# Matmuls of 512 columns issued as two of 256, with output weights moved modulo 256 bytes, in a two-layer encoder kernel

## The chip, the cores and the metric

The kernel runs on one core of a Trainium2 chip, in one launch. The metric is the device time in microseconds. Three runs of the kernel before took 1810.51, 1814.37 and 1808.48 us; their median, 1810.51 us, is the time to compare with. One execution was also profiled, and it is the source of every row shown.

## The reference

Two groups of 512 tokens of width 1024 (a prompt group and a sample group) go through the same two layers and a final norm. Layer 0 is differential attention with 8 heads, layer 1 is retention in both directions with 8 heads. Both layers have one wide input projection that also yields a gate, and one output projection. All is computed in float32.

```python
def trunk(x, ...):
    h = rms_norm(x, norm_g[0]);  x = x + diff_attention(h, da_w_in, ..., da_w_out)
    h = rms_norm(x, norm_g[1]);  x = x + bidir_retention(h, ret_w_in, ..., ret_w_out)
    return rms_norm(x, final_norm_g)

# diff_attention, per head: two softmaxes over 512 keys, a difference of them, times v,
#   rms_norm per head, times silu(gate), then o @ w_out
# bidir_retention, per head: (q k^T * decay) v forwards and backwards in chunks,
#   rms_norm per head, times silu(gate), then o @ w_out
```

## The kernel before

TensorE gets float32 precision from a rounded type (float32r): each operand is split into a high part and a low part, and each product is made of three passes, high by high, high by low and low by high (PASSES). A matmul in this text is one such pass: it loads 128 x 128 weights (the stationary operand, second argument of the call) and streams the moving operand (third argument) past them, up to 512 columns, into one bank of PSUM of 512 float32 columns. In the profile, PE is the matmul and PEld the load of its weights; each matmul has a load of its own.

The stages are these, with the lines of the profile:

- Input projections of both layers. They use a scheme with seven products in place of eight (P1 to P7), over the two groups and two halves of the depth. A Unit of kind "pair" makes its products in pair(), L599: the weights are a working tile ws of prepared projection weights, and the moving operand is a B tile of normalised activations, 512 columns wide. A Unit of kind "wide" does it the other way round, L609: the weights are a B tile, the moving operand is ws, 256 columns wide.
- Attention scores, L1116: weights are q, the moving operand is k, 512 columns. Transposes of probabilities, L1161. Attention times v, L1181: 256 columns.
- Retention: scores L1315, states L1339, near and far outputs L1359 and L1367, all of 256 columns.
- Output projections of both layers, out_step, L891: the weights are the tiles oT that hold the gated head output, the moving operand is ws with the prepared output weights, 512 columns. The very last output tile is made in two parts of 256 columns. L896 adds the product to the running x.
- Transposes for norms and layouts: L716, L815, L1028.

The work is recorded as operations with costs in a planner (Plan), which then fixes one order for each engine. The costs are written into the code and the change leaves them as they are. Each operation of TensorE is a whole group of matmuls, for instance the 12 of pair() or the 6 of out_step, and other engines wait for the end of a group. PSUM has eight banks under four tags, pj (3), sc (2), o (2) and tp (1).

SBUF is laid out in this order in each partition: small columns (pool sm), constants and B tiles (cp), the arena (ar) and working tiles (wk: raw, ws, st, os, c, e, m). The arena is one tile of 18 slots of 1024 floats, with a lead of 32 floats. slot() hands out slots, and its shift moves a tile some floats further. Tiles with the same shift lie at the same place modulo 256 bytes, since a slot is 4096 bytes. Work tiles that are not a multiple of 16 floats wide go into sm. ssf is such a tag: it has 12 columns of sums of squares that square() and x_norm() use in turn.

Of the kernel before, what the change touches and what calls it, by code (L numbers as in the profile page):

```python
# [9 lines left out]
F32 = mybir.dt.float32  # L10
F32R = mybir.dt.float32r
# [4 lines left out]
P = 128  # L16
S = 512
# [236 lines left out]
def trunk_kernel(  # L254
# [7 lines left out]
    nc = tc.nc  # L262
# [4 lines left out]
    sm = ctx.enter_context(tc.tile_pool(name="sm", bufs=1))  # L267
    cp = ctx.enter_context(tc.tile_pool(name="cp", bufs=1))
    ar = ctx.enter_context(tc.tile_pool(name="ar", bufs=1))
# [7 lines left out]
    places = {}  # L277
    cnt = [0]

    def view(pool, tag, i, size, shape, dt=F32):  # L280


        if size % 16 and pool in (cp, wk):
            pool = sm
        if (tag, i) not in places:
            places[tag, i] = pool.tile([P, size], F32, tag=f"{tag}{i}", name=f"{tag}_{i}", bufs=1)
        n = math.prod(shape[1:])
        t = places[tag, i][0:shape[0], 0:n]
        if dt != F32:
            t = t.bitcast(dt)  # L290
        if len(shape) == 3:
            t = t.rearrange("p (a b) -> p a b", a=shape[1])
        elif len(shape) == 4:
            t = t.rearrange("p (a b c) -> p a b c", a=shape[1], b=shape[2])
        return t

    def work(tag, shape, bufs, dt=F32, name=None):
        size = SIZE.get(tag, shape[1])
        return Buf(plan, tag, bufs, lambda i: view(wk, tag, i, size, shape, dt))

    arena = ar.tile([P, 18 * 1024 + 80], F32R, tag="arena", name="arena")

    def slot(n, shape, dt=F32R, shift=0):

        size = math.prod(shape[1:])
        at = None if n in (12, 13) or n >= 20 else n if n < 12 else n - 2
        if at is None:
            assert not shift  # L310
            cnt[0] += 1
            label = f"b_{cnt[0]}"
            return Buf(plan, f"b{n}", 1, lambda i: cp.tile(shape, dt, tag=f"b{n}", name=label))
        assert dt == F32R
        lo = 32 + at * 1024 + shift

        def make(i):
            t = arena[:, lo:lo + size]
            return t.rearrange("p (a b) -> p a b", a=shape[1]) if len(shape) == 3 else t
        b = Buf(plan, f"b{n}", 1, make)  # L320
        b.also = Buf(plan, f"edge{at + 1 if shift else at}", 1, None)
        return b

    def const(shape, tag, dt=F32, size=None):
        return Buf(plan, tag, 1, lambda i: view(cp, tag, i, size or math.prod(shape[1:]), shape, dt))
# [27 lines left out]
    def bank(tag, name=None):  # L353
        return Buf(plan, tag, BUFS[tag], lambda i: view(pj if tag == "pj" else sc, tag, i, S, [P, S]))
# [19 lines left out]
    def axpy(n, fn, r, w):  # L374

        plan.op("DVE", 0.13 + 0.00104 * n, fn, r, w)
# [13 lines left out]
    def pe(cost, fn, r, w, wait=0.0):  # L390
        plan.op("PE", cost, fn, r, w, wait=wait)
# [126 lines left out]
    class Unit:  # L518
# [67 lines left out]
        def product(self, op):  # L586
            which = BANK_OF[op]
            n_banks = 2 if self.wide else 1
            opens = op in OPENS
            if opens:  # L590
                self.banks[which] = [bank(self.tags[which], which) for _ in range(n_banks)]
            a, b = self.ops.pop(op), B_OF[op]
            bt = [Bop[b, k] for k in range(4)]
            reads = [q[1] for q in a] + bt

            def pair(ps, ks=range(4)):
                for k in ks:
                    for i, (u, v) in enumerate(PASSES):
                        nc.tensor.matmul(  # L599
                            ps.t, a[u][0]()[:, k, :], bt[k][:, v, :], start=(opens and k == 0 and i == 0),  # L600
                            stop=(k == 3 and i == 2), skip_group_check=True)

            def wide(ps, t):
                if self.led and op == "P1" and t == 0:
                    for j in range(NT):
                        nc.tensor.transpose(ps[:, j * P:(j + 1) * P], ident.t, ident.t)
                for k in range(4):
                    for i, (u, v) in enumerate(PASSES):
                        nc.tensor.matmul(  # L609
                            ps[:, (t % 2) * 256:(t % 2) * 256 + 256], bt[k][:, v, t * P:(t + 1) * P],  # L610
                            a[u][0]()[:, k, :], start=(opens and t % 2 == 0 and k == 0 and i == 0),
                            stop=(k == 3 and i == 2), skip_group_check=True)

            if not self.wide:
                ps = self.banks[which][0]
                if op == "P1" and self in first_units[:2]:
                    for k in range(4):
                        pe(0.7, lambda k=k: pair(ps, (k,)), reads[:2] + [bt[k]], [(ps, k)])
                else:
                    pe(2.79, lambda: pair(ps), reads, [ps])  # L620
                return
            for t in range(NT):
                ps = self.banks[which][t // 2]
                led = self.led and op == "P1" and t == 0
                pe(1.87 if led else 1.43, lambda ps=ps, t=t: wide(ps, t), reads + [ident] * led, [ps])
# [198 lines left out]
        return rr  # L824

    def new_oT(g):
        return [slot(16 + 2 * g + a, [P, 2, S], F32R, 32) for a in range(2)]

    def load_qk(src, i, shift):
        t = slot(i, [P, 2, S], F32R, shift)  # L830
# [31 lines left out]
    def out_weights(w, h, i):  # L862
        r = raw_t([P, 2, S])
        src = w[h * 256:(h + 1) * 256, i * S:(i + 1) * S].rearrange("(e p) c -> p e c", p=P)
        dma(lambda: r.t, lambda: src, [], [r], 512)
        hi, lo = ws_t([P, 2, S]), ws_t([P, 2, S])
        hi_of(1024, lambda: hi.t, lambda: r.t, [r], [hi])
        lo_of(1024, lambda: lo.t, lambda: r.t, lambda: hi.t, [r, hi], [lo])
        wsn[h, i] = (hi, lo)

    def out_step(w, h, g, t, i, o, rr, last, parts=1):


        owed[h, g] -= 1
        if (h, i) not in wsn:
            out_weights(w, h, i)
        banks = [bank("pj") for _ in range(parts)]
        u = wsn[h, i]
        x = xN[g, t]
        n = S // parts  # L880
        for p in range(parts):
            here = slice(p * n, (p + 1) * n)
            part = (x, i) if parts == 1 else (x, (i, p))

            ps = banks[p]

            def fn(here=here, ps=ps):
                m = 0
                for e in range(2):
                    for a, b in PASSES:  # L890
                        nc.tensor.matmul(ps[:, here], o[a][:, e, t * P:(t + 1) * P], u[b][:, e, here],  # L891
                                         start=(m == 0), stop=(m == 5))
                        m += 1
            pe(1.39 / parts, fn, [(o[0], t // 2), (o[1], t // 2), *u], [ps])
            half = x[:, i * S + p * n:i * S + (p + 1) * n]
            axpy(n, lambda half=half, here=here, ps=ps: nc.vector.scalar_tensor_tensor(  # L896
                half, ps[:, here], rr[:, t % 2:t % 2 + 1], half, op0=ALU.mult, op1=ALU.add),
                [ps, part, rr], [part])
            if h == NH - 1:
                last(g, t, i, half, n, part, i == 1 and p == parts - 1)  # L900
# [206 lines left out]
    def scores(i):  # L1107
        h, g, t = tiles[i]
        st[i]['s'] = []
        for j in range(2):  # L1110
            s = bank("sc")
            q, k = qk[h, g, j, 0], qk[h, g, j, 1]

            def fn(s=s, q=q, k=k):
                for n, (a, b) in enumerate(PASSES):
                    nc.tensor.matmul(s.t, q[:, a, t * P:(t + 1) * P], k[:, b, :], start=(n == 0), stop=(n == 2))  # L1116
            pe(0.7, fn, [q, k], [s])
            st[i]['s'].append(s)

# [229 lines left out]
    def av2(b, c):  # L1349
# [29 lines left out]
        if c == 0:  # L1379
            settle(h - 1, g)  # L1380
            oT[h, g] = new_oT(g)
# [71 lines left out]
    for i in range(N2 + 1):  # L1453
        if i < N2:
            b, c = chunks[i]
# [78 lines left out]
```

## Time and profile before

| what | before |
|---|---|
| median of three runs | 1810.51 us (1808.48 to 1814.37) |
| the profiled execution, first to last instruction | 1807.0 us |
| instructions | 27780 |
| matmuls, and as many loads of weights | 10299 |
| moved by DMA | 328.81 MB, mean 182 GB/s |

The span of the profiled execution leaves out what lies around its first and last instruction; the median of the runs is 3.5 us above it.

A row of the page's first part gives an engine, its busy time, its share of the span and its number of instructions. A row of a group gives line, engine, operation, what it writes and reads, the shape and the count, then the busy time in us and the mean of one in ns, then the idle time before it and what ended that. A row of the timeline gives the start in us, the length in us, the engine, line and operation, and how many instructions of one kind were merged. The end of a matmul is modelled, so lengths overlap the next row; starts are what to compare. A row of waits gives who waited for whom, the time in total, the number of times and the longest.

### The profile page before, as it was taken

How to read it: one execution, taken by the hardware profiler on the slowest of the kernel's cores; microseconds unless marked ns; L12 is line 12 of the kernel's file. 1: busy time of each engine (PE TensorE's matmuls, PEld its weight loads, DVE VectorE, ACT ScalarE, POOL GpSimd, SP SyncE). 2: the span in 40 equal slices, each digit the busy share in tenths (PEclk: the TensorE clock that was granted, in tenths of full speed). 3: DMA queues.
4: the chain of work that ended last, by engine and by line, in shares of the span. 5: the costliest groups of instructions: out<-in, count | busy, mean ns of one | idle time of the engine just before them, and what ended most of it. 6: DMA issues, size and time to landing. Idle time of an engine off the chain costs nothing.

```text
span 1807.0 us, 27780 instructions
## 1 busy us (share of the span) xinstructions
PE 1794.9 (99%) x10299; PEld 1558.1 (86%) x10299; DVE 1477.1 (82%) x2319; ACT 895.1 (50%) x1856; POOL 169.5 (9%) x323
## 2 busy tenths in 40 slices
PE   9999999999999999999999999999999999999998
PEld 6789889898988888888888888898989898888887
DVE  7958787778699888888888897787887967888887
ACT  7753444433434565554555866444434355444346
POOL 1000000000000022222322300000000000111113
PEclk9999999999999999999999999999999999999999
DMA  6444455555545685444554524464657559765662
GB/s 217 134 126 137 161 140 178 184 168 155 174 126 175 201 334 198 178 156 159 190 204 140 190 73 146 140 210 146 205 156 228 151 170 396 272 238 182 225 218 94
DMA packets 162767, 328.81 MB, mean 182 GB/s; under 512 B 12724, under 2 KB 76872, under 8 KB 162632
## 3 DMA queue, kind: packets, MB, share of 16 engines
q1 hardware_dynamic: 162304, 326.71, 54.1%
q8 instruction: 81, 1.33, 0.3%
q14 instruction: 54, 0.44, 0.1%
q10 hardware_dynamic: 328, 0.34, 0.1%
HBM read 209.55 MB, written 117.44 MB: 181 GB/s over the span
## 4 chain that ended last, share of the span: by engine, by line
PE 93%; DVE 2%; DMA 2%; ACT 2%; issue 1%; POOL 0%; SPq 0%; POOLq 0%; DVEq 0%; ACTq 0%
PE pj L599 20%; PE pj L891 19%; PE sc L599 10%; PE pj L609 10%; PE o L599 8%; PE o L1181 5%; PE sc L1116 5%; PE sc L609 5%; PE o L609 2%; PE o L1359 2%; PE tp L1161 2%; PE sc L1315 1%; PE o L1367 1%; PE tp L1339 1%; DMA raw<-in_ret_w_out_dram 1%
## 5 line engine op out<-in xcount | busy, mean ns | idle before, releaser
L891 PE MATMUL pj<-ws,arena 128*128 128x512 f32 x1542 | 391.2, 397 | 0.0
L891 PEld LDWEIGHTS pj<-ws,arena 128*128 128x128 f32 x1542 | 277.7, 188 | 52.7
L599 PE MATMUL pj<-b,ws 128*128 128x512 f32 x1080 | 265.0, 392 | 0.0
L599 PEld LDWEIGHTS pj<-b,ws 128*128 128x128 f32 x1080 | 201.4, 188 | 43.0
L403 DVE TENSOR_TENSOR ws<-st,ws 128x512 fp32r<-128x512 f32 (+1 forms) x192 | 147.9, 774 | 74.8 <-ACT ws L400 56.7
L896 DVE SCALAR_TENSOR_TENSOR b<-pj,crr,b 128x512 f32<-128x512 f32 (+1 forms) x257 | 189.9, 744 | 21.4 <-PE pj L891 21.0
L403 DVE TENSOR_TENSOR ws<-raw,ws 128x512 fp32r<-128x512 f32 (+1 forms) x164 | 141.5, 868 | 71.3 <-ACT ws L400 61.0
L400 ACT CAST ws<-st 128x512 fp32r<-128x512 f32 (+1 forms) x192 | 132.4, 693 | 121.4 <-PE pj L599 36.4
L599 PE MATMUL sc<-arena,ws 128*128 128x512 f32 x768 | 186.8, 392 | 0.0
L599 PE MATMUL o<-arena,ws 128*128 128x512 f32 x744 | 180.0, 393 | 1.1 <-ACT m L385 0.6
L599 PEld LDWEIGHTS sc<-arena,ws 128*128 128x128 f32 x768 | 144.0, 188 | 31.3
L400 ACT CAST ws<-raw 128x512 fp32r<-128x512 f32 (+1 forms) x164 | 125.7, 772 | 87.0 <-PE o L599 45.0
L599 PEld LDWEIGHTS o<-arena,ws 128*128 128x128 f32 x744 | 138.4, 188 | 31.7 <-DVE arena L463 1.4
L599 PE MATMUL pj<-arena,ws 128*128 128x512 f32 x648 | 160.3, 392 | 0.4 <-DVE arena L463 0.4
L599 PEld LDWEIGHTS pj<-arena,ws 128*128 128x128 f32 x648 | 120.8, 188 | 26.7 <-DVE arena L463 0.7
L1134 ACT ACTIVATE b<-sc,nm 128x512 f32<-128x512 f32 x128 | 88.0, 689 | 66.9 <-DVE nm L1124 66.5
L636 ACT COPY c<-pj 128x512 f32<-128x512 f32 x104 | 60.9, 586 | 119.7 <-PE pj L599 66.4
L609 PE MATMUL pj<-ws,b 128*128 128x256 f32 x960 | 116.8, 276 | 0.0
L609 PEld LDWEIGHTS pj<-ws,b 128*128 128x128 f32 x960 | 113.2, 188 | 0.7
L1116 PE MATMUL sc<-arena 128*128 128x512 f32 x384 | 101.2, 395 | 0.3 <-ACT b L1134 0.3
L1181 PEld LDWEIGHTS o<-arena 128*128 128x128 f32 x768 | 93.1, 188 | 2.7
L1181 PE MATMUL o<-arena 128*128 128x256 f32 x768 | 93.7, 278 | 0.0
(207 smaller groups left out, 2855.9 us busy)
## 6 DMA issues: line engine op xcount, KB each, us to landing
qk<-os SPq DMA_DIRECT2D x192, 256.0 KB, 3.6
arena<-qk SPq DMA_DIRECT2D x96, 512.0 KB, 5.8
raw<-in_da_w_in_dram SPq DMA_DIRECT2D x64, 512.0 KB, 5.1
v<-os SPq DMA_DIRECT2D x64, 512.0 KB, 4.3
arena<-v SPq DMA_DIRECT2D x64, 512.0 KB, 4.1
raw<-in_ret_w_in_dram SPq DMA_DIRECT2D x48, 512.0 KB, 4.8
os<-g SPq DMA_DIRECT2D x32, 512.0 KB, 7.4
g<-e SPq DMA_DIRECT2D x48, 256.0 KB, 4.6
```

Of the source, the lines that this page charges most:

```text
L400: act(n, lambda: nc.scalar.copy(dst(), src()), r, w)
L403: dve(n, lambda: nc.vector.tensor_tensor(dst(), src(), hi().bitcast(F32), op=ALU.subtract), r, w)
L599: nc.tensor.matmul(ps.t, a[u][0]()[:, k, :], bt[k][:, v, :], start=(opens and k == 0 and i == 0), stop=(k == 3 and i == 2), skip_group_che ...
L609: nc.tensor.matmul(ps[:, (t % 2) * 256:(t % 2) * 256 + 256], bt[k][:, v, t * P:(t + 1) * P], a[u][0]()[:, k, :], start=(opens and t % 2 == ...
L636: act(S, lambda c=c, ps=ps: nc.scalar.copy(c.t, ps.t), [ps], [c])
L891: nc.tensor.matmul(ps[:, here], o[a][:, e, t * P:(t + 1) * P], u[b][:, e, here], start=(m == 0), stop=(m == 5))
L896: axpy(n, lambda half=half, here=here, ps=ps: nc.vector.scalar_tensor_tensor(half, ps[:, here], rr[:, t % 2:t % 2 + 1], half, op0=ALU.mult ...
L1116: nc.tensor.matmul(s.t, q[:, a, t * P:(t + 1) * P], k[:, b, :], start=(n == 0), stop=(n == 2))
L1134: act(840, lambda j=j, s=s, m=m: nc.scalar.activation(p[:, j, :], s.t, AF.Exp, bias=m.t, accum_out=sm[:, 2 * j + n:2 * j + n + 1]), [s, m] ...
L1161: nc.tensor.transpose(tp[:, j * P:(j + 1) * P], p[:, 0, j * P:(j + 1) * P], ident.t)
L1181: nc.tensor.matmul(o[:, e * 256:(e + 1) * 256], v[b][:, j, e * P:(e + 1) * P], aT[a][:, j, :], start=(n == 0), stop=(n % 12 == 11), skip_g ...
L1359: nc.tensor.matmul(o[:, e * 256:(e + 1) * 256], v_[v][:, 2 * c + j, e * P:(e + 1) * P], a_[:, u, j * 256:(j + 1) * 256], start=(e == 0 and ...
```

## The change

There are three edits of matmuls, one of places and one that makes room.

In pair(), out_step() and scores(), each matmul of 512 columns is issued as two of 256, one after the other, with the same weights and the two halves of the moving operand, into the two halves of the same bank. Only the first of them opens the bank. Each loads its weights again. The eight matmuls that run before the first work keep their 512 columns.

The tiles oT get a shift of 64 floats in place of 32, and the arena grows by 64 floats, that is 256 bytes. The 12 columns ssf are packed in one tile of 32 columns, which takes 128 bytes in place of 12 times 32, so that sm shrinks by 256 bytes. Constants, B tiles and the arena's start move by 256 bytes, and everything behind the arena stays where it was. Modulo 256 bytes only the tiles oT and the small columns behind ssf lie elsewhere.

```diff
         if size % 16 and pool in (cp, wk):
             pool = sm
+            if tag == "ssf":
+                if tag not in places:
+                    places[tag] = sm.tile([P, 16 + 16], F32, tag=tag, name=tag, bufs=1)
+                return places[tag][:, i:i + 1]
...
-    arena = ar.tile([P, 18 * 1024 + 80], F32R, tag="arena", name="arena")
+    arena = ar.tile([P, 18 * 1024 + 144], F32R, tag="arena", name="arena")
...
                 for k in ks:
                     for i, (u, v) in enumerate(PASSES):
-                        nc.tensor.matmul(
-                            ps.t, a[u][0]()[:, k, :], bt[k][:, v, :], start=(opens and k == 0 and i == 0),
-                            stop=(k == 3 and i == 2), skip_group_check=True)
+                        for c in range(2):
+                            here = slice(c * 256, (c + 1) * 256)
+                            nc.tensor.matmul(
+                                ps[:, here], a[u][0]()[:, k, :], bt[k][:, v, here],
+                                start=(opens and k == 0 and i == 0 and c == 0),
+                                stop=(k == 3 and i == 2), skip_group_check=True)
...
     def new_oT(g):
-        return [slot(16 + 2 * g + a, [P, 2, S], F32R, 32) for a in range(2)]
+        return [slot(16 + 2 * g + a, [P, 2, S], F32R, 64) for a in range(2)]
...
                 for e in range(2):
                     for a, b in PASSES:
-                        nc.tensor.matmul(ps[:, here], o[a][:, e, t * P:(t + 1) * P], u[b][:, e, here],
-                                         start=(m == 0), stop=(m == 5))
+                        for c0 in range(here.start, here.stop, 256):
+                            nc.tensor.matmul(
+                                ps[:, c0:c0 + 256], o[a][:, e, t * P:(t + 1) * P], u[b][:, e, c0:c0 + 256],
+                                start=(m == 0 and c0 == here.start), stop=(m == 5), skip_group_check=True)
                         m += 1
...
                 for n, (a, b) in enumerate(PASSES):
-                    nc.tensor.matmul(s.t, q[:, a, t * P:(t + 1) * P], k[:, b, :], start=(n == 0), stop=(n == 2))
+                    for c in range(2):
+                        here = slice(c * 256, (c + 1) * 256)
+                        nc.tensor.matmul(s[:, here], q[:, a, t * P:(t + 1) * P], k[:, b, here],
+                                         start=(n == 0 and c == 0), stop=(n == 2), skip_group_check=True)
```

## The prediction

> **What bounds the kernel now.** I read the page first, then the groups of TensorE by form, then TensorE's waits, then its timeline, because the question is how fast one matmul follows another.
>
> ```profile
> span 1807.0 us, 27780 instructions
> PE 1794.9 (99%) x10299; PEld 1558.1 (86%) x10299; DVE 1477.1 (82%) x2319; ACT 895.1 (50%) x1856; POOL 169.5 (9%) x323
> PEclk9999999999999999999999999999999999999999
> PE 93%; DVE 2%; DMA 2%; ACT 2%; issue 1%; POOL 0%; SPq 0%; POOLq 0%; DVEq 0%; ACTq 0%
> q8 instruction: 81, 1.33, 0.3%
> ```
>
> TensorE is busy from end to end at the full granted clock, and 93% of the chain that ended last is its own work. Its longest waits, with one for a memset at the very start, are tiny:
>
> ```profile
> PE sc L1010 <- DVE minus L411: 1.4, 1, 1.4
> PE tp L1028 <- DVE arena L463: 1.0, 2, 0.7
> ```
>
> So the time is a sum of steps from one matmul's start to the next one's. The "mean ns of one" in a group is no such step: it covers the whole passage of one matmul, and matmuls overlap. What the groups give is the counts:
>
> ```profile
> L891 PE MATMUL pj<-ws,arena 128*128 128x512 f32 x1530 | 389.8, 398 | 0.0
> L599 PE MATMUL pj<-b,ws 128*128 128x512 f32 x1080 | 265.0, 392 | 0.0
> L599 PE MATMUL sc<-arena,ws 128*128 128x512 f32 x768 | 186.8, 392 | 0.0
> L599 PE MATMUL o<-arena,ws 128*128 128x512 f32 x744 | 180.0, 393 | 1.1 <-ACT m L385 0.6 <-DVE arena L463 0.3
> L599 PE MATMUL pj<-arena,ws 128*128 128x512 f32 x648 | 160.3, 392 | 0.4 <-DVE arena L463 0.4
> L1116 PE MATMUL sc<-arena 128*128 128x512 f32 x384 | 101.2, 395 | 0.3 <-ACT b L1134 0.3
> L599 PE MATMUL sc<-b,ws 128*128 128x512 f32 x120 | 29.1, 391 | 0.0
> L891 PE MATMUL pj<-ws,arena 128*128 128x256 f32 x12 | 1.6, 280 | 0.0
> ```
>
> L599 has 1080 + 768 + 744 + 648 + 120 = 3360 matmuls of 512 columns, L891 1530 and L1116 384: 5274 are split, and 5274 matmuls, each with its own load of weights, are added.
>
> **The step of a 512 against two of 256.** In the timeline the start of the next row less the start of a row, over the row's count, is the step. Two long unbroken stretches, each by its first and last row and the row after:
>
> ```profile
> 450.94 5.63 PE L609 MATMUL o<-ws,arena 128*128 128x256 f32 x48
> ...
> 472.72 5.61 PE L609 MATMUL pj<-ws,b 128*128 128x256 f32 x48
> 478.16 2.91 PE L599 MATMUL pj<-arena,ws 128*128 128x512 f32 x12
> 486.38 2.91 PE L599 MATMUL o<-arena,ws 128*128 128x512 f32 x12
> ...
> 625.08 1.53 PE L599 MATMUL pj<-arena,ws 128*128 128x512 f32 x6
> 626.46 0.86 PE L1116 MATMUL sc<-arena 128*128 128x512 f32 x3
> ```
>
> L609: 240 matmuls in 478.16 - 450.94 = 27.22 us, 113.4 ns each. L599: 612 in 626.46 - 486.38 = 140.08 us, 228.9 ns each. Two of 256 columns at L609's step are 226.8 ns, 2.1 less than one of 512. That is the small thing this change can win, and it is multiplied by thousands. But a 256 also leaves less time for the load of the next weights, and other lines of 256 show that the step isn't always 113.4:
>
> ```profile
> 640.45 2.92 PE L599 MATMUL pj<-b,ws 128*128 128x512 f32 x12
> 643.21 2.89 PE L1181 MATMUL o<-arena 128*128 128x256 f32 x24
> 645.93 0.85 PE L1116 MATMUL sc<-arena 128*128 128x512 f32 x3
> 650.87 3.01 PE L891 MATMUL pj<-ws,arena 128*128 128x512 f32 x12
> 653.72 2.99 PE L1181 MATMUL o<-arena 128*128 128x256 f32 x24
> 656.55 0.86 PE L1116 MATMUL sc<-arena 128*128 128x512 f32 x3
> 1548.49 0.86 PE L1339 MATMUL tp<-arena 128*128 128x256 f32 x6
> 1549.19 0.87 PE L1315 MATMUL sc<-arena 128*128 128x256 f32 x6
> 1549.89 1.54 PE L891 MATMUL pj<-ws,arena 128*128 128x512 f32 x6
> 1551.27 1.52 PE L1359 MATMUL o<-arena 128*128 128x256 f32 x12
> 1552.63 0.84 PE L1367 MATMUL o<-arena,b 128*128 128x256 f32 x6
> 1553.31 1.55 PE L891 MATMUL pj<-ws,arena 128*128 128x512 f32 x6
> 1554.70 0.38 PE L815 MATMUL tp<-ident,m 128*128 128x128 f32 x2
> ```
>
> L1181 takes 2.72 us for 24 in one group (113.3 ns) and 2.83 in another (117.9). L1339 and L1315 take 0.70 for 6 (116.7), L1359 1.36 for 12 and L1367 0.68 for 6 (113.3 both). The last of L891, already of 256 columns, show (1.6 - 0.28) / 11 = about 120 ns. Beside this I set where each line's weights begin, modulo 256 bytes, by the allocation of the program: 32 for L609, L1359 and L1367 (all fast), 96 for L1181 and L1339 (fast or slow), 160 for L1315 and L891 (slow). The moving operand's place (32, 96 or 224) doesn't sort them. So I read two steps of a stream of 256s, a short one of 113.4 and a long one of about 117.7 ns, and the weights' place decides which one holds.
>
> **The change part by part.**
>
> *Weights of L891.* The tiles that new_oT makes start 32 floats further, and the arena itself starts 256 bytes earlier. Their place goes from 160 to 32 modulo 256; the moving operand stays at 224. That is exactly L609's pair, so I take 113.4 ns. The 512 of today:
>
> ```profile
> 688.76 1.54 PE L1116 MATMUL sc<-arena 128*128 128x512 f32 x6
> 690.14 2.92 PE L891 MATMUL pj<-ws,arena 128*128 128x512 f32 x12
> 692.90 0.60 PE L1161 MATMUL tp<-ident,b 128*128 128x128 f32 x4
> ```
>
> 12 in 2.76 us are 230.0; the groups of six at 1549.89 and 1553.31 take 1.38 and 1.39, 230.0 and 231.7. I take 230.5. Gain: (230.5 - 226.8) x 1530 = 5.7 us. Bounds: at 113.0 a half 6.9 us are won; at 117.7 4.9 x 1530 = 7.5 us are lost.
>
> *L1116.* Weights at 32, moving at 96, as L1359 has them. Today 1.38 us for 6, 230.0 each; gain 3.2 x 384 = 1.2 us.
>
> *L599.* Its weights are the working tiles ws, at 224 modulo 256, which the change leaves alone, and no line of 256 columns has its weights there. This is the unknown price, and the largest count: 113.4 gives 2.1 x 3360 = 7.1 us won, 117.7 gives 6.5 x 3360 = 21.8 us lost. I take 113.4. For it: where L599 follows L609, as at 478.16 and 486.38, it takes over a fast stream; and L1181's group at 643.21, behind L599, was fast, while the one at 653.72, behind L891, was slow. Against it: 32, 96, 160 grow worse in that order, and 224 is the next. It is a judgement, not a reading.
>
> *Columns of sums of squares.* Twelve tiles of one column become one of 32 columns: 128 bytes a partition in place of 384, which pays for the arena's 256 more, so that every tile behind the arena keeps its address. In the built program the order of ACT, DVE, POOL and SP is unchanged, and POOL and SP wait as before. DVE gets 14 more instructions that only wait, for events of long ago; even at the 744 ns of a whole pass of L896 (the page's group of that line) they would be 10 us of the 330 that DVE is idle.
>
> ```profile
> L896 DVE SCALAR_TENSOR_TENSOR b<-pj,crr,b 128x512 f32<-128x512 f32 (+1 forms) x257 | 189.9, 744 | 21.4 <-PE pj L891 21.0
> ```
>
> I cost them at nothing, covered by TensorE's own work. Instructions are fetched by a queue that is busy 0.3% of the time; half as many again change nothing there.
>
> *Sum.* 7.1 + 5.7 + 1.2 = 14.0 us. I hand back 1.5: a stream needs some matmuls to fall into the fast step after a change of line (L1339's six lose 3.3 ns each), and an engine that is 0.8% faster will wait a little more for DVE, which has 18% to spare. Net 12.5 us. The profiled span of 1807.0 becomes 1794.5; the median of the runs, 1810.51, is 3.5 above that span, so 1798. Own range 1792 (halves at 113.0 and L1181 always fast) to 1804 (half the gain).
>
> **The rivals.**
>
> *The long step at L599.* Loads of weights come twice as often; at 224 they end last, and L599 runs as L1315 and the slow L1181 do. The price is 21.8 us against the 6.9 that L891 and L1116 win: +15, 1825. It decides from a step of 114.5 ns at L599 upward. For it stands that the place isn't measured; against it that a fast stream stays fast. 0.22. If 224 were worse still, 120 ns as L891's last twelve, 11.1 x 3360 = 37 us are lost: 1841. 0.03.
>
> *In between.* L599 flips as L1181 does, mean 115.5: 2.1 x 3360 = 7 us lost, 6.9 won: 1810. 0.09.
>
> *The shift does nothing.* L891 stays at 117.7 because place isn't the cause: +7.5 - 7.1 - 1.2 = -0.8, 1810. The fast rows at 32 speak against it. 0.03. The Trainium skill, "TensorE: Matmul & The Clock Gate" (Step-by-step: what each phase is for), says that loading weights and streaming use two independent read ports and that the load takes no bandwidth from the running matmul. By that rule alone the shift would do nothing; L1359 against L1315 here speaks against it.
>
> *A fixed cost per matmul.* Whatever sets L599's 228.9 is per column, and each further matmul costs something, as L1181's slow groups do: half of those 6.5 ns more on all 5274 is +17, 1828. Two of 256 were cheaper than one of 512 at L609, so 0.03. The same page (Back-to-back issue gap) gives N / 2.4 + 2.5 ns for a step, by which two of 256 cost 2.5 ns more than one of 512, an estimate of 13 us for the 5274, 1824. The trace differs: 228.9 and 113.4 where the rule has 215.8 and 109.2, and the pair is cheaper.
>
> **How the numbers follow.** Forecast 0.60, rivals 0.22 + 0.03 + 0.09 + 0.03 + 0.03. A difference under 0.3% (5.4 us) can't be told from no change. Faster: 0.60. Same: in between and the idle shift, 0.12. Slower: 0.28. The range 1791 to 1826 takes in the long step; left out are the worse place, half of the fixed cost and the edges of the forecast.
>
> **What would show it.** In the new timeline the long stretch of L599's line should step at 113.4 ns (0.68 us for 6), L891's line the same, L1116's too; the busy share of the weight loads goes from 86% to nearly all, and TensorE's waits stay a few us. L599 at 0.70 to 0.71 us for 6 is the long step. I am wrong altogether if TensorE shows idle time behind DVE, or if both steps stay and the time moves.

## The result, and the profile after

| | before | after |
|---|---|---|
| median | 1809.49 us (4 runs, 1808.26 to 1814.37) | 1833.66 us (4 runs, 1832.97 to 1836.69) |
| ratio to before, 95% interval | | 1.0137 (1.0124 to 1.0150) |
| span of the profiled execution | 1807.0 us | 1831.8 us |

The changed kernel is 1.4% slower. The forecast was 1798.0 us, and its range ended at 1826. Lines have moved: L599 is now L605, L609 is L616, L891 is L899, L1116 is L1127, L1181 is L1193, L1359 is L1371, L1367 is L1379.

The page of the kernel after, its head, chain and instruction queue:

```profile
span 1831.8 us, 38342 instructions
PE 1819.5 (99%) x15573; PEld 1810.2 (99%) x15573; DVE 1480.0 (81%) x2319; ACT 895.3 (49%) x1856; POOL 169.3 (9%) x323
PEclk9999999999999999999999999999999999999999
q8 instruction: 122, 2.00, 0.5%
PE 95%; DVE 2%; DMA 1%; issue 1%; ACT 1%; POOL 0%; SPq 0%; POOLq 0%; DVEq 0%; ACTq 0%
```

TensorE's longest waits, after:

```profile
PE sc L1019 <- DVE minus L415: 1.4, 1, 1.4
PE o L1037 <- DVE b L391: 1.1, 1, 1.1
```

Nothing came in from outside TensorE. It is as busy as before at the same granted clock, its waits are of the same size, instructions are fetched by a queue that is busy 0.5% of the time, and 15573 - 10299 = 5274 matmuls were added as counted. So the 24.8 us lie in the steps. Adding up, over the whole trace, the time from each matmul's start to the next one's, and giving it to the line of the first, shows where:

| line before / after | before, us | after, us | difference | taken in the prediction |
|---|---|---|---|---|
| L599 / L605 | 774.3 | 787.8 | +13.5 | -7.1 |
| L609 / L616 (not split) | 305.7 | 309.9 | +4.2 | 0 |
| L891 / L899 | 362.1 | 363.9 | +1.8 | -5.7 |
| L1116 / L1127 | 89.8 | 91.9 | +2.1 | -1.2 |
| L1181 / L1193 (not split) | 88.4 | 89.6 | +1.2 | 0 |
| L1359 / L1371 (not split) | 43.7 | 45.3 | +1.6 | 0 |
| L1367 / L1379 (not split) | 22.2 | 22.6 | +0.4 | 0 |

The differences add up to 24.8, the whole change of the span. Lines that nobody touched pay 7.4 of it.

The timeline shows what happened inside a line (start, length, count; the step is the distance of starts over the count):

```profile
196.78 5.82 PE L616 MATMUL pj<-ws,b 128*128 128x256 f32 x48
202.44 2.99 PE L605 MATMUL o<-arena,ws 128*128 128x256 f32 x24
...
292.90 2.99 PE L605 MATMUL pj<-b,ws 128*128 128x256 f32 x24
295.72 5.62 PE L616 MATMUL pj<-ws,arena 128*128 128x256 f32 x48
301.17 2.89 PE L605 MATMUL pj<-b,ws 128*128 128x256 f32 x24
303.89 5.82 PE L616 MATMUL o<-ws,arena 128*128 128x256 f32 x48
...
490.36 5.62 PE L616 MATMUL pj<-ws,b 128*128 128x256 f32 x48
495.81 2.88 PE L605 MATMUL o<-arena,ws 128*128 128x256 f32 x24
...
633.17 1.52 PE L605 MATMUL pj<-arena,ws 128*128 128x256 f32 x12
634.53 0.85 PE L1127 MATMUL sc<-arena 128*128 128x256 f32 x6
```

From 202.44 to 295.72 L605 runs 792 matmuls in 93.28 us, 117.78 ns each. From 495.81 to 634.53 the same line, with its weights at the same place modulo 256, runs 1224 in 138.72 us, 113.33 ns each. Neither step gives way to the other while the stream lasts. L616, with weights at 32, does both too: (202.44 - 196.78) / 48 = 117.9 ns, (301.17 - 295.72) / 48 = 113.5 ns. So one line has both steps with its weights at one place, and the place alone can't be what decides. The rows suggest that it is how a stream was entered, which the experiments below test. In the rows above, L616 takes the other step than the L605 ahead of it (long to short at 295.72, short to long at 303.89), and L605 keeps the step of the L616 ahead of it. Over the trace, the change from L605 to L616 turned the step round 19 times of 23, and the change from L616 to L605 kept it 24 times of 24. As the lines alternate, an unbroken stretch then has the one step or the other by the number of changes before it. Of L605's matmuls 1781 took 112 to 115 ns and 4909 took 116 to 124; of L616's 1614 and 1069, where before 2554 of them were short and 129 long.

The same timeline where output products alternate with scores, and with the far outputs:

```profile
697.68 1.58 PE L1127 MATMUL sc<-arena 128*128 128x256 f32 x12
699.09 2.89 PE L899 MATMUL pj<-ws,arena 128*128 128x256 f32 x24
701.82 0.60 PE L1173 MATMUL tp<-ident,b 128*128 128x128 f32 x4
...
1543.83 1.58 PE L1371 MATMUL o<-arena 128*128 128x256 f32 x12
1545.24 0.86 PE L1351 MATMUL tp<-arena 128*128 128x256 f32 x6
```

L899 runs at (701.82 - 699.09) / 24 = 113.8 ns here, but L1127 at 1.41 / 12 = 117.5, and L1371, for which the prediction had 113.3, at 1.41 / 12 = 117.5 as well. The weights of all three lie at 32, which the prediction had called the good place. Over the whole trace L899 is mixed, with 1367 matmuls of 112 to 115 ns and 1609 of 116 to 124, L1127 is long in 730 of its 768, and L1371 in all of its 384.

### The profile page after: what moved, and what is told of

Read it like the earlier page. It is cut to its first block, busy times and chain, and to the rows that moved or that the text cites. A ratio compares the mean times of both kernels' runs of the same rounds, so it can differ in the third digit from the quotient of the medians.

```text
span 1831.8 us, 38342 instructions
## 1 busy us (share of the span) xinstructions
PE 1819.5 (99%) x15573; PEld 1810.2 (99%) x15573; DVE 1480.0 (81%) x2319; ACT 895.3 (49%) x1856; POOL 169.3 (9%) x323
## 4 chain that ended last, share of the span: by engine, by line
PE 95%; DVE 2%; DMA 1%; issue 1%; ACT 1%; POOL 0%; SPq 0%; POOLq 0%; DVEq 0%; ACTq 0%
PE pj L605 21%; PE pj L899 19%; PE sc L605 11%; PE pj L616 10%; PE o L605 8%; PE o L1193 5%; PE sc L1127 5%; PE sc L616 5%; PE o L1371 2%; PE o L616 2%; PE tp L1173 2%; PE sc L1327 1%; PE o L1379 1%; PE tp L1351 1%; DVE ws L407 0%
## 5 line engine op out<-in xcount | busy, mean ns | idle before, releaser
L899 PE MATMUL pj<-ws,arena 128*128 128x256 f32 x3072 | 393.1, 281 | 0.0
L899 PEld LDWEIGHTS pj<-ws,arena 128*128 128x128 f32 x3072 | 369.3, 189 | 0.1
L605 PE MATMUL pj<-b,ws 128*128 128x256 f32 x2160 | 269.3, 279 | 0.0
L605 PEld LDWEIGHTS pj<-b,ws 128*128 128x128 f32 x2160 | 259.2, 188 | 0.0
L905 DVE SCALAR_TENSOR_TENSOR b<-pj,crr,b 128x512 f32<-128x512 f32 (+1 forms) x257 | 190.2, 745 | 22.6 <-PE pj L899 21.2
L605 PE MATMUL sc<-arena,ws 128*128 128x256 f32 x1536 | 189.9, 279 | 0.0
L605 PE MATMUL o<-arena,ws 128*128 128x256 f32 x1488 | 183.6, 279 | 1.0 <-ACT m L389 0.6
L605 PEld LDWEIGHTS sc<-arena,ws 128*128 128x128 f32 x1536 | 183.7, 188 | 0.0
L605 PEld LDWEIGHTS o<-arena,ws 128*128 128x128 f32 x1488 | 177.9, 188 | 1.9 <-DVE arena L467 1.1
L605 PE MATMUL pj<-arena,ws 128*128 128x256 f32 x1296 | 162.3, 278 | 0.3 <-DVE arena L467 0.3
L605 PEld LDWEIGHTS pj<-arena,ws 128*128 128x128 f32 x1296 | 155.5, 188 | 0.7 <-DVE arena L467 0.5
L616 PE MATMUL pj<-ws,b 128*128 128x256 f32 x960 | 118.6, 278 | 0.0
L616 PEld LDWEIGHTS pj<-ws,b 128*128 128x128 f32 x960 | 114.3, 188 | 0.0
L1127 PE MATMUL sc<-arena 128*128 128x256 f32 x768 | 103.4, 281 | 0.3 <-ACT b L1146 0.3
L1127 PEld LDWEIGHTS sc<-arena 128*128 128x128 f32 x768 | 95.5, 188 | 0.7 <-ACT b L1146 0.7
L1193 PE MATMUL o<-arena 128*128 128x256 f32 x768 | 94.8, 280 | 0.0
```

The lines of the kernel that those rows point to most:

```text
L605: nc.tensor.matmul(ps[:, here], a[u][0]()[:, k, :], bt[k][:, v, here], start=(opens and k == 0 and i == 0 and c == 0), stop=(k == 3 and i ...
L616: nc.tensor.matmul(ps[:, (t % 2) * 256:(t % 2) * 256 + 256], bt[k][:, v, t * P:(t + 1) * P], a[u][0]()[:, k, :], start=(opens and t % 2 == ...
L899: nc.tensor.matmul(ps[:, c0:c0 + 256], o[a][:, e, t * P:(t + 1) * P], u[b][:, e, c0:c0 + 256], start=(m == 0 and c0 == here.start), stop=( ...
L1127: nc.tensor.matmul(s[:, here], q[:, a, t * P:(t + 1) * P], k[:, b, here], start=(n == 0 and c == 0), stop=(n == 2), skip_group_check=True)
L1193: nc.tensor.matmul(o[:, e * 256:(e + 1) * 256], v[b][:, j, e * P:(e + 1) * P], aT[a][:, j, :], start=(n == 0), stop=(n % 12 == 11), skip_g ...
```

## The experiments

All kernels here compute the whole reference. A "whole" matmul has 512 columns, a "half" is one of the two of 256 that replace it, and a "product" is the group of twelve whole matmuls that one call of pair() makes. "Short" is the step of 113.3 ns for 256 columns, "long" the step of 117.8. Sums by line are made as in the table above and are named by the lines of before; rows of a timeline have the lines of their own kernel. The ratios are formed from all runs, so they can differ a little from the ratio of the medians.

**One edit at a time.** Four kernels take the change apart, with hunks of the change itself. e1_pair_only is the kernel before with the hunk of pair(). e2_pair_whole is the change without that hunk. e3_place_only is the kernel before with ssf in one tile, the longer arena and the shift, and no split; e4_split_old_place is the change without these (the hunk of ssf is the one shown with the change):

```diff
...
-    arena = ar.tile([P, 18 * 1024 + 80], F32R, tag="arena", name="arena")
+    arena = ar.tile([P, 18 * 1024 + 144], F32R, tag="arena", name="arena")
...
-        return [slot(16 + 2 * g + a, [P, 2, S], F32R, 32) for a in range(2)]
+        return [slot(16 + 2 * g + a, [P, 2, S], F32R, 64) for a in range(2)]
```

> Only pair() is split, everything else as before. Theory A (a stream of 256s has a short step of 113.4 ns and a long one of 117.7 that both hold by themselves; a change of line hands the step on or flips it): the split line has a mix of both, mean 116.6 as in the changed kernel, and L609, which is untouched, loses too, mean about 115; (2 x 116.6 - 229.0) x 3360 = 14 us and 1.5 x 2688 = 4 us, so 1828 (1820 to 1835). Theory B (the weights' place modulo 256 sets the step): the split line has the long step throughout, (235.4 - 229.0) x 3360 = 21 us, 1831, and L609 stays at 113.6 ns. Theory C (twice the instructions starve TensorE): waits without a releaser at TensorE, and L609 as before.

> The changed kernel with pair() left at 512 columns. Theory A: the rest of the loss, 24 - 18 = 6 us, so about 1815; L609 back at 113.6 ns since each L599 product of 512s stands before it; L1359 and L1367 long as in the changed kernel. Theory B: the out_step line, its weights now at 32, is short throughout, and 5.7 + 1.2 us are won, 1803.

> Only the places: oT moved to 32 modulo 256, ssf packed, no matmul split. Theory A and C: 512s do not feel the place, 1809 to 1811. Theory B: the twelve last 256s of L891 are short, 0.05 us, else the same.

> All three splits, but oT and ssf where they were before, weights of L891 at 160 modulo 256. Theory A: the place does not set the step, only what a change of line does with it: the out_step line has a mix of both steps, time within 10 us of the changed kernel, 1824 to 1844. Theory B: the out_step line is long throughout (117.7 ns against 115.7 in the changed kernel), 4 x 1530 = 6 us more, 1840, and L609 keeps what it has in the changed kernel.

| | median, us (before 1808.60) | ratio, 95% interval | L599 | L609 | L891 | L1116 | L1359 |
|---|---|---|---|---|---|---|---|
| e1_pair_only | 1826.42 | 1.0093 (1.0078 to 1.0108) | 784.3 | 312.7 | 362.2 | 89.9 | 43.7 |
| e2_pair_whole | 1816.36 | 1.0045 (1.0030 to 1.0060) | 773.9 | 305.7 | 363.9 | 91.9 | 45.2 |
| e3_place_only | 1813.94 | 1.0029 (1.0017 to 1.0040) | 774.8 | 305.9 | 365.5 | 89.7 | 45.1 |
| e4_split_old_place | 1833.97 | 1.0143 (1.0128 to 1.0158) | 780.6 | 312.7 | 367.9 | 91.7 | 45.2 |

The two parts of the change add up: 1.0093 and 1.0045 to 1.0137. Splitting pair() alone costs 10.0 us in L599 and 7.0 in L609, which it does not touch; theory A had 14 and 4, and with 1828 and 1815 it was near the times of e1_pair_only and e2_pair_whole, where theory B had 1831 with L609 unchanged, and 1803. The places alone are not free, which neither theory had: the matmuls of 512 columns at L891 lose 3.4 us, and L1359, whose own operands stay where they were modulo 256, turns long. With the splits, the new places give L891 4.0 us (367.9 against 363.9; 1609 of its matmuls long against 2535 at the old place, nearly as theory B had that line), but L599 and L609 together take 4.4 more, and the whole time stays the same, where theory B had 1840. The timeline of e3_place_only, whose L1363 is L1359 of before:

```profile
1551.49 1.55 PE L895 MATMUL pj<-ws,arena 128*128 128x512 f32 x6
1552.88 1.57 PE L1363 MATMUL o<-arena 128*128 128x256 f32 x12
1554.30 0.87 PE L1371 MATMUL o<-arena,b 128*128 128x256 f32 x6
```

Twelve of L1363 take 1.42 us, 118.3 ns, where before they took 1.36 behind the same six output products. The trace shows what turned L1359: of its 29 groups behind L891 in before, the 28 that came behind a last step of 235 or 236 ns were short and the one behind 226 was long; in e3_place_only 28 came behind 230 or 231 and were long, and one behind 235 was short. So the places changed the steps of L891, and with its last step went the step of the line behind it. Whether the packed ssf had a share in the 0.3% was not tried by itself.

**Twice the same weights, or 512 as a fresh start?** The first two passes of pair() both load the high part of ws, and the third the low part. So in the change four of every six halves follow one with the same weights. In e5_halves_outside it is two of six, not none as its expectation says. In e6_last_whole the twelfth matmul of each product stays whole, and in e7_last_split only the twelfth is split, 280 matmuls in all, so that the halves are few and L609 stays as it is. First the edit of e5_halves_outside against the hunk of the change, then those of e6_last_whole and e7_last_split:

```diff
-                    for i, (u, v) in enumerate(PASSES):
-                        for c in range(2):
-                            here = slice(c * 256, (c + 1) * 256)
+                    for c in range(2):
+                        here = slice(c * 256, (c + 1) * 256)
+                        for i, (u, v) in enumerate(PASSES):
```

```diff
+                        n = 512 if k == 3 and i == 2 else 256
+                        for c0 in range(0, 512, n):
```

```diff
+                        n = 256 if k == 3 and i == 2 else 512
+                        for c0 in range(0, 512, n):
```

> pair() alone is split, in another order: for each k, the three passes of the left half and then the three of the right, so that no matmul is followed by one with the same weights. Theory A (each step holds by itself and is handed on at a change of line): again a mix of 113.4 and 117.7 in the split line and in L609, 1815 to 1835. Theory D (loading the same weights a second time at once makes the long step): the long step is gone from the split line, (229.0 - 226.8) x 3360 = 7 us won, 1801.

> pair() alone is split, but the last of the twelve matmuls of each product (k = 3, last pass) stays whole: 280 of 512 columns and 6160 of 256. Theory A, with a matmul of 512 columns as what sets the stream back to the short step: L609 is short again (305 to 306 us in all, against 312.7 in e1), and the split line is short except behind transposes, 280 x 0.231 + 6160 x 0.1134 = 763 us against 774: 1798. If a 512 sets the step back for L609 but not for the split line's own next product: 280 x 0.231 + 6160 x 0.1177 = 790, 1824. Theory B (the weights' place sets the step): 1824 as well, but then e1 would have had no short steps.

> The kernel before with only the last of the twelve matmuls of each product of pair() issued as two of 256: 280 matmuls more. Theory A: what stands before L609 is no longer a 512 but a 256, which hands the long step on; L609, which is untouched, goes from 113.7 to up to 117.7 ns, up to 2688 x 4 = 11 us, so 1813 to 1820, nearly all of it in a line that the edit does not touch. Theories B and D: at most 280 x 7 = 2 us, 1808 to 1811, L609 as before.

Against 1808.68 us for before, e5_halves_outside took 1825.81 (1.0088, 1.0068 to 1.0109), as much as e1_pair_only. By itself that leaves a share of repeated weights. Two other rows rule them out as the cause: the stretches of 792 long and 1224 short halves in the changed kernel repeat their weights in the same order, and L609, in which no neighbour has the same weights (its passes load high, low, high, and then the next k), is long in 2500 of 2688 in e7_last_split below. e6_last_whole took 1835.40 (1.0143, 1.0127 to 1.0158), more than either time expected: a whole matmul does not end the long step. Its timeline, whose L601 is L599 of before, and where 22 halves and one whole matmul are merged in a row:

```profile
505.77 2.99 PE L601 MATMUL sc<-arena,ws 128*128 128x256 f32 x23
508.60 3.00 PE L601 MATMUL pj<-b,ws 128*128 128x256 f32 x23
511.44 0.75 PE L601 MATMUL pj<-arena,ws 128*128 128x256 f32 x5
```

A product takes 2.83 us, which is 22 x 117.8 ns and 235 for the whole one. Among the steps of its lone whole matmuls 218 had long halves on both sides, and in 8 cases short halves became long behind a step of 225 or 226. e7_last_split took 1821.41 (1.0067, 1.0051 to 1.0083), a little above the 1813 to 1820 of theory A. In its timeline, eleven whole matmuls and two halves are a row of x13:

```profile
454.86 2.96 PE L601 MATMUL pj<-b,ws 128*128 128x512 f32 x13
457.66 5.81 PE L612 MATMUL o<-ws,arena 128*128 128x256 f32 x48
463.31 5.82 PE L612 MATMUL sc<-ws,arena 128*128 128x256 f32 x48
```

L612, L609 of before, steps at (463.31 - 457.66) / 48 = 117.7 ns. No instruction of that line was changed, and it went from 305.7 to 316.3 us, with 2500 of its 2688 long. So the step of a line depends on what ran just before it. The same trace shows how the halves themselves are entered, 280 times: of the first halves, all 110 behind a whole matmul with a step of 231 or 232 ns took 113 or 114, all 150 behind 225 to 230 took 117 to 120, and all 20 behind 233 or 234 took 119 or 120.

**Halves only inside a stretch.** Before, the wide products came in behind products of twelve whole matmuls, and nearly all were short. In e8_inner_split a product is split only when its neighbours are pair or wide products and a pair product follows, so the last product ahead of L609 stays whole. In e9_steered, in stretches that begin behind transposes, the second product is whole but for its twelfth matmul, in order to move the point at which the halves begin. plan.before and plan.behind are the kinds of the operations ahead and behind in TensorE's final order, and plan.run counts the pair products since a stretch began.

```diff
+                n = 256 if len(ks) == 4 and plan.before in ("pair", "wide") and plan.behind == "pair" else 512
```

```diff
+                split = len(ks) == 4 and plan.run > 0 and plan.behind == "pair"
...
+                        n = 256 if split and (plan.run > 1 or (k, i) == (3, 2)) else 512
```

> pair() is split only inside a stretch: a product whose neighbour before is a product of pair() or a wide one and whose neighbour behind is a product of pair(). Next to transposes or scores, and right before a wide product, the twelve matmuls stay whole; 2532 of 3360 are split. Theory A (a stream keeps its step through 256s and 512s alike, and only a change of line can flip it; twelve 512s end where the kernel before ends them): L609 short, 305 to 306 us in all; where a stretch of split products is entered from a short L609 it is short, 113.4 ns. If all stretches are short 2532 x 2.2 ns = 5.6 us are won: 1803. The first stretch (888 matmuls) and those behind transposes may be long: then 1804 to 1812. Theory B (place): the split stretches are long, +16 us, 1825.

> As e8, but where a stretch of split products starts behind transposes, the splitting starts one matmul earlier: the second product has eleven whole matmuls and its twelfth split, in place of twelve whole ones. In e8 the long stretches (888 matmuls from 51.4 us, 816 from 1060.3 us) follow a 512 with a step of 226 or a wait; eleven whole ones end on a step of 231 or 232. Theory A: a stream enters 256s short if the 512 before it had a step of 231 or 232, so both stretches turn short, about 1700 x 4.4 ns = 7.5 us less than e8 with the small stretch at 1043.5 left as it is: 1801 to 1804, faster than both kernels. If the entry does not decide, the two stretches stay long and the time is e8's, 1808.

Neither can be told from before: 1807.85 against 1808.72 us (0.9997, 0.9988 to 1.0006), and 1810.26 against 1808.67 (0.9997, 0.9988 to 1.0006; its runs fall into 1804 to 1807 and 1810 to 1811). But L609 was back at 305.7 us, and the stretches fell in two kinds. The timeline of e8_inner_split, whose L609 is L599 of before, one stretch of each:

```profile
202.96 2.89 PE L609 MATMUL o<-arena,ws 128*128 128x256 f32 x24
...
290.00 2.91 PE L609 MATMUL pj<-b,ws 128*128 128x512 f32 x12
...
1060.34 2.99 PE L609 MATMUL sc<-arena,ws 128*128 128x256 f32 x24
...
1156.44 2.92 PE L609 MATMUL pj<-b,ws 128*128 128x512 f32 x12
```

Behind wide products, 768 halves in 87.04 us, 113.33 ns; behind whole products that follow transposes, 816 in 96.10, 117.77. All eight stretches that begin behind wide products were short in both kernels, and the three others long in both. The steering of e9_steered did not do what it was meant to: its three stretches began behind whole matmuls with steps of 226 and 229, not 231 or 232, as the long ones of e8_inner_split at 1043.52 and 1060.34 had. So its 1801 to 1804 was not put to the test. What the runs left was a rule to try: whole matmuls step in a cycle of about 226, 229, 232, and halves that begin behind a step of 231 or 232 are short, behind the others long.

**The rule, tried.** Behind a short L609 the cycle always stands at the same place, so there the entry can be chosen. e10_behind_wide splits only the eight stretches that begin there. e11_ten_whole and e12_eleven_whole keep ten and eleven whole matmuls in the first product of each of them (the second diff, with 11 for 10 in the latter). Here plan.run is 0 outside these stretches; in the second diff it is 1 at their first product and 2 behind it.

```diff
+                self.run = dict(pair=self.run, wide=1).get(getattr(fn, "kind", ""), 0)
...
+                split = len(ks) == 4 and plan.run > 0 and plan.behind == "pair"
...
+                        n = 256 if split else 512
```

```diff
+                self.run = dict(pair=2 * (self.run > 0), wide=1).get(getattr(fn, "kind", ""), 0)
...
+                        n = 256 if split and (plan.run > 1 or 3 * k + i >= 10) else 512
```

> The kernel before with pair() split into halves only in the eight stretches of products that begin right behind a wide product (L609); the last product of each stretch and all other stretches stay whole. 1656 matmuls are split, 3312 halves. Theory (the step is handed on, and behind a short L609 the halves come in short): all eight stretches at 113.34 ns, 228.9 - 226.7 = 2.2 ns won on each of 1656, 3.7 us: 1805 against 1808.7, with a narrow spread of runs, since no stretch is entered from transposes. Rival (the step of a stretch is drawn anew in each execution): some stretches long, 4.4 ns on each of their halves, so 1805 to 1819 with a spread of several us.

> As e10_behind_wide, but in the first product of each stretch ten matmuls stay whole and only the last two are split: 80 splits fewer, 0.2 us. The steps of whole matmuls behind L609 go 228, 229, 232, 226, 229, 232 and so on, so after ten the halves begin behind a step of 226 and not of 231 or 232. Theory (the halves take the step from where the cycle of three stands when they begin): the stretches run at 117.78 ns, 3152 x 4.44 = 14.0 us more than e10_behind_wide, 1819; if the wide products behind them take the long step over too, up to 10 us more. Rival (the line, the weights' place or the position in the program sets the step): as e10_behind_wide, within 1 us.

> As e11_ten_whole, with eleven whole: the halves begin behind a step of 229. Theory: long too, since the long stretches seen so far began behind 226 or 229: 1819 or more. If only 226 leads to the long step, as e10_behind_wide. Rival (place, line or position): as e10_behind_wide, within 1 us.

| | median, us (before 1808.90) | ratio, 95% interval | L599 | L609 | halves of L599 short / long |
|---|---|---|---|---|---|
| e10_behind_wide | 1804.63 | 0.9975 (0.9965 to 0.9985) | 770.2 | 305.7 | 3312 / 0 |
| e11_ten_whole | 1819.20 | 1.0056 (1.0042 to 1.0070) | 786.6 | 305.7 | 0 / 3152 |
| e12_eleven_whole | 1816.66 | 1.0040 (1.0026 to 1.0054) | 779.5 | 308.6 | 1420 / 1716 |

The page of e10_behind_wide, and its longest stretch in the timeline (L610 is L599 of before in all three):

```profile
span 1802.8 us, 31092 instructions
PE 1789.7 (99%) x11955; PEld 1621.8 (90%) x11955; DVE 1477.3 (82%) x2319; ACT 895.2 (50%) x1856; POOL 170.0 (9%) x323
...
484.88 2.88 PE L610 MATMUL o<-arena,ws 128*128 128x256 f32 x24
...
620.88 1.54 PE L610 MATMUL pj<-b,ws 128*128 128x512 f32 x6
```

The same stretch of e11_ten_whole (the first row is ten whole matmuls and four halves):

```profile
491.95 2.92 PE L610 MATMUL o<-arena,ws 128*128 128x512 f32 x14
494.70 2.99 PE L610 MATMUL sc<-arena,ws 128*128 128x256 f32 x24
...
633.21 1.55 PE L610 MATMUL pj<-b,ws 128*128 128x512 f32 x6
```

And of e12_eleven_whole two stretches, the first at 201.47:

```profile
201.47 2.99 PE L610 MATMUL sc<-arena,ws 128*128 128x256 f32 x24
...
289.10 2.91 PE L610 MATMUL pj<-b,ws 128*128 128x512 f32 x12
...
494.96 2.88 PE L610 MATMUL sc<-arena,ws 128*128 128x256 f32 x24
...
628.24 1.53 PE L610 MATMUL pj<-b,ws 128*128 128x512 f32 x6
```

e10_behind_wide runs 1200 halves in 136.00 us, 113.33 ns each. In e11_ten_whole the same products run 1176 halves in 138.51 us, 117.78 each; the two kernels differ there in ten matmuls at the head. In e12_eleven_whole 744 halves take 87.63 us, 117.78 each, at 201.47, and 1176 take 133.28, 113.33 each, at 494.96. Its first stretch began behind a step of 230, its fourth behind one of 231: ahead of that one L609 had been long, and the whole matmuls behind a long L609 step 235, 231, 237, 232, 231, 226, 229 and so on, where behind a short one they step 228, 229, 232, 226, 229, 232. The eleventh then falls on 231 and not on 229. L609 has values of its own: it was long behind whole products that ended at 226 or 227, short behind those that ended at 230, 231 or 236. So the time missed the 1819 expected, while the rule for the halves held stretch by stretch. Over e8 to e12, every one of the 24 stretches that began right behind a short wide product was short, both that began behind 231 or 232 were short, and all 19 that began behind 225 to 230 were long (one more, in e8_inner_split at 51.42, began behind a stall and was long). That halves are long behind any whole matmul, short only behind L609, is a rival that e10_behind_wide and e11_ten_whole leave; the two short stretches of e12_eleven_whole and the 110 short entries of e7_last_split speak against it. The rival that line, place or position sets the step is out: e11_ten_whole changes none of them, and costs 14.6 us.

e10_behind_wide beats both kernels, before by a ratio of 0.9975 and by 4.3 us in the medians, where 1656 x 2.2 ns made 3.7; L599 alone went from 774.3 to 770.2. Its nine runs lie within 1 us.

## Why the prediction was wrong

**What bounds the kernel** was right: the time is a sum of steps, before and after, and the added instructions, waits and fetches cost nothing that can be seen. The busy share of the loads of weights went from 86% to 99%, as forecast.

**The two steps** were right, 113.3 and 117.8 ns, and hardly anything else occurs in a long stream.

**The step that failed** is "the weights' place decides which one holds". It came from rows that all had a history of their own: L609 stood at 32 and was short, but 22 of the 23 times that it followed L599 directly, the last step of L599 was 230 or 231. With the history changed, L609 was long at 32 (e7_last_split), L1359 was long at 32 (e3_place_only and after), and L605 was both at 224. What the runs showed in its place is that the step is settled where a stream is entered, by the step that ran just before: ten whole matmuls kept at the head of each of eight stretches made the kernel 14.6 us longer (e11_ten_whole against e10_behind_wide), with the same places and lines. A row that contradicted the reading stood in the prediction: L1181, at 96, was put down as a place where either step may hold. It was not sorted by the line before it either, as the prediction's two groups suggested, one behind L599 and one behind L891. This group behind L891 is short, at 2.73 us for 24:

```profile
719.37 2.90 PE L1181 MATMUL o<-arena 128*128 128x256 f32 x24
722.10 1.54 PE L1116 MATMUL sc<-arena 128*128 128x512 f32 x6
```

Of the 22 groups of L1181 behind L891, the 13 behind a last step of 231 were short and the 9 behind 237 or 238 long. So the trace of before held the answer, in the last step ahead of each group. Which value makes which step differs from one pair of lines to the next: 231 led to the short step here and, in e3_place_only, to the long one at L1359.

**L599.** Taken at 113.4, -7.1 us; it was +13.5, with 4909 of its 6720 halves long. The long ones cost 4909 x 4.4 = 21.6 against all short. That L599 "takes over a fast stream" from L609 was true as far as the step was kept (24 of 24), but it didn't help, because L616 was itself long in 14 of these.

**L891 and L1116.** The gains of 5.7 and 1.2 us were losses of 1.8 and 2.1. The shift did help the split L891, by 4.0 us against e4_split_old_place, but still left 1609 of its matmuls long, and L1116 ran long in 730 of 768 at its "good" place. The 120 ns that the prediction read for the last twelve of L891 come from rounded figures of the page; the trace has 118.0, so there is no third step.

**What was costed at nothing.** Lines that the change leaves alone lost 4.2 + 1.2 + 1.6 + 0.4 = 7.4 us, and the shift without any split (with ssf packed) cost 0.29%. The prediction held that a line has its step from its own operands, so it had no term for what an edit does to the next line. It handed back 1.5 us for changes of line, as if a stream fell into the short step by itself after a few matmuls. L609 does so in before, with some five steps of 116 to 123 ns and then 113 or 114; but halves that were entered long stayed long, over as many as 1180 (e11_ten_whole).

**From the span to the time.** The prediction added 3.5 us to the profiled span. That was the distance to the median of three runs, two of them long ones for this kernel (1810.51 and 1814.37); wherever a run has both, its time is 1.7 to 2.0 us above its own span. Its own sum thus makes 1796.4 and not 1798, a small error beside the miss.

**The rivals.** The long step at L599, 1825, was the nearest in kind, with the right price for a long half. But it stopped at L599: it had 21.8 us lost there, where 13.5 were, 6.9 won at L891 and L1116, where 3.9 were lost, and nothing elsewhere, where 7.4 were lost. Its time lay 9 us short. The rival of a fixed cost, 1828, was nearer in time and wrong in its mechanism: with the step kept short, the split wins, as e10_behind_wide shows. The rule of the Trainium skill, "TensorE: Matmul & The Clock Gate" (Step-by-step: what each phase is for), that the load of weights takes no bandwidth from the running matmul, had been set against the shift. Whether a load takes bandwidth is not shown by any run; the places (with ssf packed) changed the time by 0.29%, so they do act on the steps, but no place fixed one.

**What stays open.** Which part of TensorE holds the two steps isn't shown by any trace here; nor is why the change from L605 to L616 mostly turns the step and the change back keeps it, why the same last step leads to the short step on one line and the long one on another, nor how a place acts on the steps of whole matmuls. The runs of one kernel differ too: most of before lie at 1808.0 to 1809.3 us, some at 1810.2 to 1811.1 and a few at 1814.3 to 1814.4. In e8_inner_split and e9_steered the runs spread over 5 to 7 us, where those of e10_behind_wide, without stretches behind transposes, lie within 1. A stretch of 800 or 900 halves that is short in some executions would account for 4 us, but only one execution of each was profiled, and the counts by stretch are those of that execution.

## What to carry to other kernels

Where TensorE is busy from end to end, read the step of each stretch and not of each line: a line can have two, and the one that it has may come from what ran before it, so that an edit to one line is paid in the next. Sort the stretches by the last step ahead of them before you sort them by anything else. A price read from rows is good for the history that these rows had; before multiplying a gain of 2 ns by thousands, look for the same shape behind another line. And where a change of shape wins only from one entry, as here behind L609, apply it there alone: 1656 splits won 4.3 us where 5274 lost 24.2.

## What the runs showed of the hardware

A stream of 256 columns in this float32r form with a load of weights for each matmul has two steps, each of which holds for a thousand matmuls: 113.33 ns, as 113, 113 and 114, 340 for three, and 117.78 ns, 353.3 for three. Whole matmuls go in a cycle of 226, 229 and 232. Which step a stream of halves behind whole matmuls took was settled at its first one, by the place in that cycle at which it began: behind 231 or 232 short, behind 225 to 230 long, in the first halves of 280 products of e7_last_split (there also long behind 233 or 234) and in 21 stretches of e8 to e12. Ten whole matmuls at the head of a stretch, which ended at a step of 226, turned 1180 halves behind them from short to long. At a change of line the last step ahead sorts too, with other values: for L1359 behind L891 235 or 236 led to the short step and 230 or 231 to the long one. A lone whole matmul among long halves took up to 235 ns and left them long.
